# Two transformer blocks on one core: down and output products with the activations stationary, and token-major norms

## The chip, the cores and the metric

The kernel runs on one core of one Trainium2 chip. The metric is device time in microseconds (us), the median of several executions. A profile is one more execution, taken by the hardware profiler, and its span runs from the first to the last instruction of the core.

## What is computed

The reference runs 256 tokens of width 1024 through two blocks of two layers each, in float32. A layer of the first block has three sublayers (feed-forward, mixer, feed-forward), each followed by a residual and a layer norm; a layer of the second has a mixer and a convolutional feed-forward.

```python
# first block, l = 0, 1
y = swiglu(modulate(x, mod[:, 0, 0], mod[:, 0, 1]), ffn_w13[l, 0], ffn_w2[l, 0])
x = layer_norm(ALPHA * x + 0.5 * (1 + mod[:, 0, 2])[:, None, :] * y, ln_g[l, 0], ln_b[l, 0])
y = token_mixer(modulate(x, ...), w_in[l], w_out[l], ...)
x = layer_norm(ALPHA * x + (1 + mod[:, 1, 2])[:, None, :] * y, ln_g[l, 1], ln_b[l, 1])
...
# second block, l = 0, 1 (h = layer_norm_2(x, ln_in_g, ln_in_b) ahead of it)
mix = jnp.concatenate([da_o, hg_o, mx_o], axis=-1) @ w_out
x = layer_norm_2(DEEPNORM_ALPHA * x + mix, ln1_g, ln1_b)
u = depthwise_conv_centred(x @ w_up, conv_w, conv_b)
gate, val = jnp.split(u, 2, axis=-1)
return layer_norm_2(DEEPNORM_ALPHA * x + (jax.nn.silu(gate) * val) @ w_down, ln2_g, ln2_b)
```

`layer_norm` takes mean and variance over the 1024 features of a token, then a gain and a bias by feature. The feed-forward width is 2816.

## The kernel before

**Layout.** Activations are feature-major: a tile of 128 partitions holds 8 groups (KT) of 128 features by 256 tokens (S). Weights come from memory in chunks of 128 x 2048 (1 MB), issued by SyncE (SP in the profile) into a ring of three raw buffers, in the order in which the products take them.

**Products.** Every float32 product is three products of a shorter format: an operand is cast to a high part and the rest is its low part, and hi·hi, lo·hi and hi·lo are added up in PSUM. `Chunk.hi` (L247, ScalarE) and `Chunk.lo` (L255, VectorE) split a weight chunk; `split` (L530, L531) splits activations; `mm3` (L425 to L427) issues the three products. In all of these 128 x 128 of the weights is stationary and 256 tokens of activations move past it, so that features come out on partitions. `gemm_a` (L550 to L553) is the same for the projections into a sublayer, with its own order. One projection group per mixer (L852) moves 408 columns.

**Down.** The class `Down` (L267) makes the product that ends a sublayer: the feed-forward's second matrix (11 chunks, `ffn` L556), the mixers' output matrix (4 chunks in `mixer1` L828, 6 in `mixer2`). A chunk gives 8 feature groups x 2 halves x 3 products of 256 columns, 48 matmuls, into 4 PSUM banks `y`, each bank holding two feature groups. The last two chunks are taken group by group, so that the groups finish one after the other.

**The norm.** `norm` (L706) adds `y`, times the gate in the first block, to the scaled residual `xa` (VectorE, L714 or L716). `sums` (L667) makes the sums over features: ScalarE squares (L680), VectorE adds up the first feature groups (L684, L685), and TensorE adds up across partitions and the remaining groups with a matrix of 1/1024 (L688; plain float32, two array passes per matmul). Mean and 1/deviation then stand on all partitions for each token. `scaled` (L721) subtracts the mean (L698) and multiplies (L723) group by group on VectorE; `make_xf` (L477) makes of each group, with gain, bias and the next sublayer's modulation as scale and bias by partition, the high part `xh` and the full `xm` (both ScalarE, L480) and the low part `xl` (VectorE, L484). The next sublayer's products start on group 0 as soon as it is there. Between the blocks two norms follow each other (`norm_again` L732). `residual` (L746, called by `keep` early in the next sublayer) makes `xa` from the normed tile on ScalarE (L741). The last norm writes out through `dump` (L1641).

**Work beside the norms.** `filler` and `kv_chunk` (L617 to L645) hold eight chunks of products of `mem` with a later mixer's weights. `program` (L1651) gives one chunk (48 matmuls) to each of the norms (0,0), (0,1), (0,2), (1,0), (1,1) and (2,1), and two to (1,2), the double norm. (l,s) is the norm behind sublayer s of layer l of the first block; (2,1) is the one behind the second block's first feed-forward. The two norms behind `mixer2` and the last norm have none. A scheduler sets the order in which each engine gets its instructions from priorities; the diff does not spell it out.

Of the kernel before, what the change touches and what calls it, by code (L numbers as in the profile page):

```python
# [10 lines left out]
F32 = mybir.dt.float32  # L11
# [7 lines left out]
P = 128  # L19
D = 1024  # L20
# [50 lines left out]
def _consts():  # L71
# [17 lines left out]
    out = [[("ident", np.eye(P)), ("mean", np.full((P, P), 1.0 / D)), ("ones", np.ones((P, P))), ("zeros", np.zeros((P, 8)))],  # L89
# [97 lines left out]
def host_pack(i):  # L187
# [10 lines left out]
    a["xT"] = np.ascontiguousarray(i["x"][0].T.reshape(KT, P, S).transpose(1, 0, 2).reshape(P, KT * S))  # L198
    a["c"] = np.ascontiguousarray(i["c"])
# [67 lines left out]
class Down:  # L267


    def __init__(self, net, y, n):  # L270
        self.net, self.y, self.n, self.i = net, y, n, 0

    def add(self, c, hh, hl):
        i, n = self.i, self.n
        self.i += 1
        if i == n - 2:
            self.kept = (i, c, hh, hl)
        for f in range(KT):
            if i < n - 1 and (f < 4 or i < n - 2):
                self.part(f, i, c, hh, hl)  # L280
            elif i == n - 1:
                if f >= 4:
                    self.part(f, *self.kept)
                self.part(f, i, c, hh, hl)

    def part(self, f, i, c, hh, hl):
        for kk in range(2):
            self.net.mm3(self.y[f // 2][:, (f % 2) * S:(f % 2 + 1) * S], *c(kk * D + f * P, P), hh[kk], hl[kk],
                         i == 0 and kk == 0 and f % 2 == 0, i == self.n - 1 and kk == 1 and f % 2 == 1)
# [20 lines left out]
class Net:  # L310
    def __init__(self, ctx, tc, a, soff, off):
# [9 lines left out]
        self.xap = ent(tc.tile_pool(name="xap", bufs=1))  # L321
# [33 lines left out]
    def constants(self, pool, j):  # L355

        nc = self.nc
        for kind, dt in (("consts", F32), ("masks", U8), ("sels", F32R)):
# [6 lines left out]
            if dt == F32:  # L365
                nc.sync.dma_start(t, src)
            else:
                with self.tc.tile_pool(name="mskf", bufs=1) as tmp:
                    f = tmp.tile([P, n], F32, name="mskf")[:m]
                    nc.sync.dma_start(f, src)  # L370
                    nc.vector.tensor_copy(t, f)
# [105 lines left out]
    def make_xf(self, f, src, A, B, xh, xl, between=lambda: None, late=False):  # L477
        nc = self.nc
        t = self.temp("xm")
        to = lambda t: self.pin(nc.scalar.activation(out=t, in_=src[:, f], func=AF.Identity, scale=A[:, f:f + 1], bias=B[:, f:f + 1]), late)  # L480
        to(xh[:, f])
        between()
        to(t)
        self.pin(nc.vector.tensor_tensor(out=xl[:, f], in0=t, in1=xh[:, f].bitcast(F32), op=ALU.subtract), late)  # L484

    def make_x(self, src, A, B, each):
        xh, xl = self.new_x()
        for f in range(KT):
            each(f)
            self.make_xf(f, src, A, B, xh, xl)  # L490
            self.between(f)
        return xh, xl

    def start(self, c1, w, ada):
# [6 lines left out]
        with ExitStack() as ctx:  # L501
# [3 lines left out]
            for f in range(KT):  # L505
# [16 lines left out]
                self.make_xf(f, r, mod[:, 8:16], mod[:, 0:8], xh, xl, rest, True)  # L522
# [4 lines left out]
        return r, xh, xl, small  # L527
# [28 lines left out]
    def ffn(self, wa, wb, xh, xl, conv, extra, fill, made=()):  # L556

        nc = self.nc
        with ExitStack() as ctx:
# [7 lines left out]
            for g in range(NG):  # L567
# [36 lines left out]
                extra(g, side)  # L604
                if fill and g == 3:
                    mem = self.memory(side, *(F.tile([P, KT, S], F32R, bufs=1, tag=t, name=t) for t in ("memh", "meml")))
            down.add(*held.pop())
            yield y, pwt, self.filler(mem, F, pwt) if fill else no_fill
# [58 lines left out]
    def sums(self, r, each, st, direct=6):  # L667


        nc = self.nc  # L670
        v, mm = nc.vector, nc.tensor.matmul
        new = self.temp
        self.table(RSQRT)
        s1, s2 = new("s1"), new("s2")
        st = st()
        parts = [(s1, s2)]
        for f in range(KT):
            each(f)
            q = s2 if f == 0 else new("sq")
            nc.scalar.activation(out=q, in_=r[:, f], func=AF.Square)  # L680
            if f >= direct:
                parts.append((r[:, f], q))
            elif f > 0:
                v.tensor_tensor(out=s1, in0=s1 if f > 1 else r[:, 0], in1=r[:, f], op=ALU.add)  # L684
                v.tensor_tensor(out=s2, in0=s2, in1=q, op=ALU.add)  # L685
        for i, p in enumerate(parts):
            for j in range(2):
                mm(st[:, j * S:(j + 1) * S], self.cs("mean"), p[j], start=i == 0 and j == 0, stop=i == len(parts) - 1 and j == 1)  # L688
        self.between(-1)
        t, y, u, mean = new("lnt"), new("lny"), new("lnu"), new("s1")  # L690
        nc.scalar.activation(out=t, in_=st[:, :S], func=AF.Square)
        v.scalar_tensor_tensor(out=t, in0=st[:, S:], scalar=LN_EPS, in1=t, op0=ALU.add, op1=ALU.subtract)
        v.tensor_copy(mean, st[:, :S])
        nc.scalar.activation(out=y, in_=t, func=AF.Abs_reciprocal_sqrt)

        def center(f):
            if f < KT:
                self.pin(v.tensor_tensor(out=r[:, f], in0=r[:, f], in1=mean, op=ALU.subtract))  # L698
        center(0)
        nc.scalar.activation(out=u, in_=y, func=AF.Square)  # L700
        v.scalar_tensor_tensor(out=u, in0=u, scalar=-0.5, in1=t, op0=ALU.mult, op1=ALU.mult)
        center(1)
        v.scalar_tensor_tensor(out=y, in0=u, scalar=1.5, in1=y, op0=ALU.add, op1=ALU.mult)
        return y, center

    def norm(self, y, gate, res, st, fill, A=None, B=None, done=lambda r, f: None):  # L706

        v = self.nc.vector
        r = self.rp.tile([P, KT, S], F32, tag="r", name="r")

        def each(f):
            yf = y[f // 2][:, (f % 2) * S:(f % 2 + 1) * S]
            if gate is None:
                v.tensor_tensor(out=r[:, f], in0=yf, in1=res[:, f], op=ALU.add)  # L714
            else:
                v.scalar_tensor_tensor(out=r[:, f], in0=yf, scalar=gate[:, f:f + 1], in1=res[:, f], op0=ALU.mult, op1=ALU.add)  # L716
        rs = self.sums(r, each, st)
        fill()
        return r, self.scaled(r, *rs, A, B, lambda f: done(r, f))

    def scaled(self, r, rs, center, A, B, done=lambda f: None):  # L721
        def each(f):
            self.nc.vector.tensor_tensor(out=r[:, f], in0=r[:, f], in1=rs, op=ALU.mult)  # L723
            center(f + 2)
            done(f)
        if A is None:
            for f in range(KT):
                each(f)
            return None
        return self.make_x(r, A, B, each)  # L730

    def norm_again(self, r, g, b, st, fill, A, B):  # L732

        each = lambda f: self.nc.scalar.activation(out=r[:, f], in_=r[:, f], func=AF.Identity, scale=g[:, f:f + 1], bias=b[:, f:f + 1])
        rs = self.sums(r, each, st, 3)
        fill()
        return self.scaled(r, *rs, A, B)

    def affine(self, src, A, B, dst, f, act):
        if act:  # L740
# [1034 lines left out]
```

## Time and profile before

| what | us |
|---|---|
| median of 3 runs | 2069.29 (2068.16 to 2069.84) |
| profiled execution, its own time | 2064.67 |
| its span | 2062.9 |
| TensorE (PE) busy | 2011.7 of the span, 16076 instructions |
| VectorE (DVE) busy | 1596.4, 3028 instructions |
| ScalarE (ACT) busy | 1160.7, 1918 instructions |
| mean granted TensorE clock | 0.996 of full speed |
| DMA | 400.72 MB, 194 GB/s in the mean |

The profiled execution is 4.6 us under the median. Its span leaves 1.8 us of its time outside. Matmuls are pipelined, so a matmul's own duration is longer than the distance to the next one; that distance, start to start, is what a matmul costs. The row of PE clock digits on the page is 9 throughout, in 40 slices of 52 us.

### The profile page before, as it was taken

To read this page: it belongs to the slowest core of one execution; us is meant where nothing else is said; L and a number is where in the kernel's file an instruction comes from. 1 tells how busy PE (TensorE), PEld (TensorE's weight loads), DVE (VectorE), ACT (ScalarE), POOL (GpSimd) and SP (SyncE) were. 2 spreads that over 40 slices of the span, in tenths; PEclk is the share of its full clock that TensorE was granted. 3 is DMA by queue.
4 is the path that set the end of the run, shared out by engine and by line. 5 is a ranking of instruction groups with operands and counts; after the bars stand their busy time and mean duration, and the time that the engine had idled before them with its cause. 6 is when DMAs were issued, how large, how long until landed. Compare 5 with 4: busy or idle time off the path is not lost.

```text
span 2062.9 us, 39007 instructions
## 1 busy us (share of the span) xinstructions
PE 2011.7 (98%) x16076; PEld 1962.6 (95%) x16076; DVE 1596.4 (77%) x3028; ACT 1160.7 (56%) x1918; POOL 10.4 (1%) x18
## 2 busy tenths in 40 slices
PE   8999999999999999999999999999999999999997
PEld 7999989899999999999999999999899999989997
DVE  7877898987778775997886459786877697868775
ACT  4644734674447444735574448564765585648554
POOL 0000000000000000000000000000000000000000
PEclk9999999999999999999999999999999999999999
DMA  9785444478875783433377533434465343336541
GB/s 392 302 340 220 169 144 154 146 265 309 306 266 220 305 314 139 169 129 109 122 268 276 182 128 138 141 124 164 158 224 185 108 166 133 117 123 212 198 164 40
DMA packets 59445, 400.72 MB, mean 194 GB/s; under 512 B 6786, under 2 KB 8450, under 8 KB 12291
## 3 DMA queue, kind: packets, MB, share of 16 engines
q1 hardware_dynamic: 59266, 398.23, 52.9%
q8 instruction: 126, 2.06, 0.4%
q14 instruction: 53, 0.43, 0.1%
HBM read 395.05 MB, written 3.15 MB: 193 GB/s over the span
## 4 chain that ended last, share of the span: by engine, by line
PE 90%; DVE 5%; ACT 3%; issue 1%; DMA 0%; SPq 0%; ACTq 0%; DVEq 0%
PE pw L425 14%; PE pw L427 14%; PE pw L426 14%; PE y L425 6%; PE y L427 6%; PE y L426 6%; PE pw L550 3%; PE pw L551 3%; PE pw L553 3%; PE py L1529 2%; PE py L1113 1%; PE py L1107 1%; PE pw L778 1%; PE pw L780 1%; PE pw L779 1%; PE pz L425 1%
## 5 line engine op out<-in xcount | busy, mean ns | idle before, releaser
L255 DVE TENSOR_TENSOR lo<-raw,hi 128x1024 fp32r<-128x1024 f32 (+1 forms) x588 | 705.8, 1214 | 285.3 <-ACT hi L247 283.3
L247 ACT CAST hi<-raw 128x1024 fp32r<-128x1024 f32 (+1 forms) x588 | 601.6, 1041 | 436.7 <-PE pw L427 307.3
L425 PE MATMUL pw<-xh,hi 128*128 128x256 f32 x2536 | 724.2, 286 | 2.3 <-DVE zo L925 2.3
L427 PE MATMUL pw<-xl,hi 128*128 128x256 f32 x2536 | 720.7, 284 | 0.0
L426 PE MATMUL pw<-xh,lo 128*128 128x256 f32 x2536 | 720.3, 284 | 0.0
L425 PEld LDWEIGHTS pw<-xh,hi 128*128 128x128 f32 x2536 | 485.7, 192 | 4.8 <-DVE zo L925 2.4
L426 PEld LDWEIGHTS pw<-xh,lo 128*128 128x128 f32 x2536 | 485.7, 192 | 0.6
L427 PEld LDWEIGHTS pw<-xl,hi 128*128 128x128 f32 x2536 | 485.7, 192 | 0.5
L425 PE MATMUL y<-hh,hi 128*128 128x256 f32 x1056 | 296.3, 283 | 2.3 <-ACT hh L530 1.8
L426 PE MATMUL y<-hh,lo 128*128 128x256 f32 x1056 | 296.9, 283 | 0.5 <-DVE lo L255 0.5
L427 PE MATMUL y<-hl,hi 128*128 128x256 f32 x1056 | 296.3, 282 | 0.1
L425 PEld LDWEIGHTS y<-hh,hi 128*128 128x128 f32 x1056 | 200.9, 191 | 3.2 <-ACT hh L530 2.2
L426 PEld LDWEIGHTS y<-hh,lo 128*128 128x128 f32 x1056 | 201.6, 191 | 0.7 <-DVE lo L255 0.7
L427 PEld LDWEIGHTS y<-hl,hi 128*128 128x128 f32 x1056 | 201.4, 191 | 0.3 <-DVE hl L531 0.3
L453 DVE CUSTOM_DVE_ANT_0 raw<-raw,cb 128x1024 f32<-128x1024 f32 x144 | 171.7, 1219 | 18.7 <-DMA raw<-ada 12.7
L550 PE MATMUL pw<-xh,hi 128*128 128x256 f32 x464 | 118.3, 290 | 18.4 <-ACT xh L480 15.9
L551 PE MATMUL pw<-xh,lo 128*128 128x256 f32 x464 | 116.8, 288 | 0.0
L550 PEld LDWEIGHTS pw<-xh,hi 128*128 128x128 f32 x464 | 89.5, 197 | 21.6 <-ACT xh L480 18.5
L551 PEld LDWEIGHTS pw<-xh,lo 128*128 128x128 f32 x464 | 89.5, 197 | 0.3 <-DVE lo L255 0.2
L530 ACT CAST hh<-h 128x512 fp32r<-128x512 f32 x66 | 40.9, 620 | 68.6 <-DVE h L594 68.0
L553 PE MATMUL pw<-xl,hi 128*128 128x256 f32 x464 | 77.7, 286 | 0.4 <-DVE xl L484 0.4
L553 PEld LDWEIGHTS pw<-xl,hi 128*128 128x128 f32 x464 | 65.4, 193 | 1.2 <-DVE xl L484 1.2
(450 smaller groups left out, 3029.6 us busy)
## 6 DMA issues: line engine op xcount, KB each, us to landing
raw<-w SPq DMA_DIRECT2D x132, 1024.0 KB, 6.8
raw<-ada SPq DMA_DIRECT2D x72, 1024.0 KB, 4.9
raw<-win SPq DMA_DIRECT2D x62, 1024.0 KB, 4.9
raw<-wup SPq DMA_DIRECT2D x44, 1024.0 KB, 5.1
raw<-wdn SPq DMA_DIRECT2D x22, 1024.0 KB, 4.9
raw<-wo SPq DMA_DIRECT2D x12, 1024.0 KB, 4.9
raw<-wkv SPq DMA_DIRECT2D x8, 1024.0 KB, 4.9
raw<-wout SPq DMA_DIRECT2D x8, 1024.0 KB, 5.0
```

The lines of the kernel that those rows point to most:

```text
L247: self.net.pin(self.net.nc.scalar.copy(t[:, :m], self.raw[len(self.parts)]), late)
L255: self.net.pin(self.net.nc.vector.tensor_tensor(out=t[:, :m], in0=self.raw[i], in1=h[:, :m].bitcast(F32), op=ALU.subtract), late)
L425: mm(out, wh, xh, start=start, stop=False)
L426: mm(out, wl, xh, start=False, stop=False)
L427: mm(out, wh, xl, start=False, stop=stop)
L453: i = nc.vector.tensor_tensor_reduce(out=t[:, j * D:(j + 1) * D], in0=t[:, j * D:(j + 1) * D], in1=self.cb, scale=1.0, scalar=0.0, op0=ALU ...
L530: self.pin(self.nc.scalar.copy(hi, src), late)
L550: mm(o, wh, xh[:, k], start=k == 0 and n == 0, stop=False)
L551: mm(o, wl, xh[:, k], start=False, stop=False)
L553: mm(p[:, n * S:(n + 1) * S], wh, xl[:, k], start=False, stop=k == KT - 1 and n == 1)
L778: mm(out, ah, wh, start=k == 0, stop=False)
L1529: mm(p[:, (2 * j + c) * P:(2 * j + c + 1) * P], k, r, start=True, stop=True)
```

## The change

`Down` is turned round: the activations (128 features x 128 tokens) are stationary, and the weights move 512 columns at a time, so `y` comes out token-major, one PSUM bank for 128 tokens x 512 features. A chunk is 24 matmuls. The last two chunks are taken so that tokens 0 to 127 finish first (`y` banks 0 and 1), then bank 2, then bank 3.

The norm becomes token-major. The residual `r` is one resident tile of 128 x 2 x 1024. VectorE multiplies by the gate, adds and takes statistics (`bn_stats`, `bn_aggr`); VectorE and ScalarE share the normalising; TensorE transposes 16 blocks of 128 x 128 per norm back to feature-major ("flips", L744); ScalarE makes `xh` (L768) from PSUM, VectorE `xm` (L769) and `xl` (L770). The residual's gain and bias are now rows that lie along the free dimension, so they are loaded as rows broadcast to 128 partitions (`rows`, 1 MB, ten of them), and the gates are written to memory and read back broadcast (`row`, 512 KB, six of them). The input `x` is loaded token-major as well (1 MB). The constant 1/1024 goes, and the identity is used. `sums`, `scaled`, `norm_again`, `make_x` and `affine` go.

```diff
 class Down:
     def add(self, c, hh, hl):
         i, n = self.i, self.n
         self.i += 1
-        if i == n - 2:
-            self.kept = (i, c, hh, hl)
-        for f in range(KT):
-            if i < n - 1 and (f < 4 or i < n - 2):
-                self.part(f, i, c, hh, hl)
...
+        self.kept.append((i, c, hh, hl))
+        if i < n - 2:
+            for t in range(2):
+                self.part(t, (0, 1))
+        elif i == n - 1:
+            self.part(0, (0, 1))
+            for j in range(2):
+                self.part(1, (j,))
+        if i != n - 2:
+            self.kept = []
+
+    def part(self, t, columns):
+        mm = self.net.nc.tensor.matmul
+        for i, c, hh, hl in self.kept:
+            for kk in range(2):
+                h, l = (x[kk][:, t * P:(t + 1) * P] for x in (hh, hl))
+                w = [(self.y[2 * t + j], *c(kk * D + j * 512, 512)) for j in columns]
+                for y, wh, _ in w:
+                    mm(y, h, wh, start=i == 0 and kk == 0, stop=False)
+                for y, _, wl in w:
+                    mm(y, h, wl, start=False, stop=False)
+                for y, wh, _ in w:
+                    mm(y, l, wh, start=False, stop=i == self.n - 1 and kk == 1)
...
+    def normal(self, y, gate, again=None):
...
+        for t in range(2):
+            r = self.r[:, t]
+            bn = self.stats()
+            for j in range(2):
+                c, p = slice(j * 512, (j + 1) * 512), y[2 * t + j]
+                if gate is not None:
+                    v.tensor_tensor(out=p, in0=p, in1=gate[:, c], op=ALU.mult)
+                v.tensor_tensor(out=r[:, c], in0=p, in1=r[:, c], op=ALU.add)
+                v.bn_stats(out=bn[:, j], in_=r[:, c])
+            mean, rs, nb = self.deviation(bn)
...
+            for j in range(4):
+                x = r[:, j * 256:(j + 1) * 256]
+                if j % 2 == 0:
+                    v.tensor_scalar(out=x, in0=x, scalar1=mean, scalar2=rs, op0=ALU.subtract, op1=ALU.mult)
+                else:
+                    sc.activation(out=x, in_=x, func=AF.Identity, scale=rs, bias=nb)
+
+    def feature_major(self, banks, fill, each):
...
+        for f in range(KT // 2):
+            flip(0, f)
+        fill()
+        ps += [bank(k) for k in banks[2:]]
+        for f in range(KT // 2, KT):
+            flip(0, f)
         for f in range(KT):
...
+            flip(1, f)
+        for f in range(KT):
+            each(f, ps[f // 2][:, f % 2 * S:(f % 2 + 1) * S])
...
+        def each(f, p):
+            t = self.temp("xm")
+            a, b = A[:, f:f + 1], B[:, f:f + 1]
+            nc.scalar.activation(out=xh[:, f], in_=p, func=AF.Identity, scale=a, bias=b)
+            nc.vector.tensor_scalar(out=t, in0=p, scalar1=a, scalar2=b, op0=ALU.mult, op1=ALU.add)
+            nc.vector.tensor_tensor(out=xl[:, f], in0=t, in1=xh[:, f].bitcast(F32), op=ALU.subtract)
+            self.between(f)
...
+    def residual(self, rows):
 
         v = self.nc.vector
...
+            v.scalar_tensor_tensor(out=r, in0=r, scalar=ALPHA, in1=rows[0], op0=ALU.mult, op1=ALU.mult)
+            v.scalar_tensor_tensor(out=r, in0=rows[1], scalar=ALPHA, in1=r, op0=ALU.mult, op1=ALU.add)
```

`deviation` (L692) is `bn_aggr` (L698), a reciprocal square root on ScalarE (L699) and four VectorE operations on one column (L700 to L703), for each half of the tokens.

TensorE, the first down product of a feed-forward, before (`hh`, `hl`: the activations' parts; `hi`, `lo`: the weights'; the last name is the moving operand's or the stationary one's, the shape is the moving one's):

```order
L425 MATMUL y<-hh,hi 128x256 x4
L426 MATMUL y<-hh,lo 128x256
L427 MATMUL y<-hl,hi 128x256
L425 MATMUL y<-hh,hi 128x256
L426 MATMUL y<-hh,lo 128x256
L427 MATMUL y<-hl,hi 128x256
L425 MATMUL y<-hh,hi 128x256
```

The same place with the change:

```order
L300 MATMUL y<-hi,hh 128x512 x2
L302 MATMUL y<-lo,hh 128x512 x2
L304 MATMUL y<-hi,hl 128x512 x2
L300 MATMUL y<-hi,hh 128x512 x2
L302 MATMUL y<-lo,hh 128x512 x2
```

The operands have changed places, there are half as many matmuls, and each is twice as wide.

TensorE at the norm behind the first mixer, before (`py<-mem` is the filler; `py<-s` the sums with 1/1024):

```order
L427 MATMUL pw<-mhl,hi 128x256
L688 MATMUL py<-s_4843,consts_841 128x256
L425 MATMUL py<-mem,hi 128x256
L426 MATMUL py<-mem,lo 128x256
L427 MATMUL py<-mem,hi 128x256
```

And with the change (`pt<-consts,res` are the flips):

```order
L304 MATMUL pw<-hi,mhl 128x512
L300 MATMUL pw<-hi,mhl 128x512
L302 MATMUL pw<-lo,mhl 128x512
L304 MATMUL pw<-hi,mhl 128x512
L744 MATMUL pt<-consts_795,res 128x128 x4
L441 MATMUL py<-mem,hi 128x256
L442 MATMUL py<-mem,lo 128x256
L443 MATMUL py<-mem,hi 128x256
```

Four flips of the first 128 tokens stand between the last product and the filler; the other twelve stand behind the filler's 48 matmuls, ahead of the next projection.

VectorE in the same norm, before, from the reciprocal of the deviation on:

```order
L703 SCALAR_TENSOR_TENSOR lny<-lnu,lny 128x256
L723 TENSOR_TENSOR r<-r,lny 128x256
L698 TENSOR_TENSOR r<-r,s_4894 128x256
L723 TENSOR_TENSOR r<-r,lny 128x256
L698 TENSOR_TENSOR r<-r,s_4894 128x256
L723 TENSOR_TENSOR r<-r,lny 128x256
L484 TENSOR_TENSOR xl<-xm,xh 128x256
```

And with the change, from the end of the second half's statistics on (`lo<-raw` is the split of the next sublayer's weights):

```order
L703 SCALAR_TENSOR_TENSOR dev<-dev 128x1
L734 TENSOR_SCALAR res<-res,dev 128x256 x2
L259 TENSOR_TENSOR lo<-raw,hi 128x1024 x2
L783 SCALAR_TENSOR_TENSOR res<-res,rows 128x1024
L769 TENSOR_SCALAR xm<-pt,mab 128x256
L784 SCALAR_TENSOR_TENSOR res<-rows,res 128x1024
L770 TENSOR_TENSOR xl<-xm,xh 128x256
L769 TENSOR_SCALAR xm<-pt,mab 128x256 x2
L770 TENSOR_TENSOR xl<-xm,xh 128x256
```

The residual's two operations on the first half (L783, L784, 1024 columns each) now stand ahead of the first `xl`.

## Rows read from the trace of the kernel before

**Rows 1.** The page's busy times by engine.

```profile
PE 2011.7 (98%) x16076; PEld 1962.6 (95%) x16076; DVE 1596.4 (77%) x3028; ACT 1160.7 (56%) x1918; POOL 10.4 (1%) x18
```

**Rows 2.** The page's chain of work that ended last, share by engine.

```profile
PE 90%; DVE 5%; ACT 3%; issue 1%; DMA 0%; SPq 0%; ACTq 0%; DVEq 0%
```

**Rows 3.** Window 450:620: busy PE PEld DVE ACT POOL, clock, DMA share, GB/s.

```profile
450.00:620.00 170.00, 170.00 (x1422) 170.00 (x1421) 128.14 (x171) 82.30 (x99) 0.00 (x0) 1.00 0.79 297
```

**Rows 4.** Timeline of TensorE at 100 us: start, duration, instruction; 256 columns.

```profile
100.10 0.28 PE L426 MATMUL pw<-xh,lo 128*128 128x256 f32 x1
100.22 0.28 PE L427 MATMUL pw<-xl,hi 128*128 128x256 f32 x1
```

**Rows 5.** Timeline of TensorE at 218 us, 408 columns.

```profile
218.10 0.35 PE L852 MATMUL pw<-lo,xh 128*128 128x408 f32 x1
...
218.66 0.35 PE L852 MATMUL pw<-lo,xh 128*128 128x408 f32 x1
```

**Rows 6.** Timeline of TensorE, plain float32: sums (two passes each) and transposes.

```profile
1307.79 0.60 PE L1579 MATMUL pz<-consts,e 128*128 128x128 f32 x4
...
1447.94 0.59 PE L688 MATMUL py<-sq,consts 128*128 128x256 f32 x2
1448.37 0.59 PE L688 MATMUL py<-r,consts 128*128 128x256 f32 x2
```

**Rows 7.** Groups by line and shape: busy, mean ns | idle before, releaser.

```profile
L255 DVE TENSOR_TENSOR lo<-raw,hi 128x1024 fp32r<-128x1024 f32 x576 | 695.1, 1221 | 284.1 <-ACT hi L247 282.1
L531 DVE TENSOR_TENSOR hl<-h,hh 128x512 fp32r<-128x512 f32 x66 | 45.4, 688 | 15.5 <-ACT hh L530 15.5
L484 DVE TENSOR_TENSOR xl<-xm,xh 128x256 fp32r<-128x256 f32 x80 | 33.4, 421 | 5.7 <-ACT xm L480 5.2
L480 ACT ACTIVATE xh<-r,mab 128x256 fp32r<-128x256 f32 x40 | 23.9, 597 | 8.9 <-DVE r L723 8.9
L1600 DVE TENSOR_SCALAR mx<-mx 128x2 f32<-128x2 f32 x16 | 2.5, 163 | 0.0
```

**Rows 8.** Timeline of TensorE: last down product and first projection at (0,0).

```profile
203.71 0.28 PE L427 MATMUL y<-hl,hi 128*128 128x256 f32 x1
...
211.94 0.35 PE L852 MATMUL pw<-hi,xh 128*128 128x408 f32 x1
```

**Rows 9.** The same two at (0,1).

```profile
422.49 0.28 PE L427 MATMUL pw<-mhl,hi 128*128 128x256 f32 x1
...
432.34 0.39 PE L550 MATMUL pw<-xh,hi 128*128 128x256 f32 x1 [1.02 <-ACT kvo L642]
```

**Rows 10.** The same two at (1,2), the double norm.

```profile
1233.58 0.28 PE L427 MATMUL y<-hl,hi 128*128 128x256 f32 x1
...
1254.86 0.38 PE L550 MATMUL pw<-xh,hi 128*128 128x256 f32 x1 [1.23 <-ACT xh L480]
```

**Rows 11.** The same two behind the first mixer2, a norm without filler.

```profile
1446.52 0.28 PE L427 MATMUL pw<-xl,hi 128*128 128x256 f32 x1
...
1453.81 0.58 PE L550 MATMUL pw<-xh,hi 128*128 128x256 f32 x1 [4.42 <-ACT xh L480]
```

**Rows 12.** Busy time by window there.

```profile
1452.00:1454.00 2.00, 0.19 (x1) 0.19 (x2) 1.97 (x6) 0.84 (x2) 0.00 (x0) 0.51 0.00 0
1454.00:1458.90 4.90, 4.90 (x24) 4.90 (x25) 4.90 (x14) 4.90 (x9) 0.00 (x0) 0.50 0.00 0
```

**Rows 13.** The same two at (2,1).

```profile
1647.67 0.28 PE L427 MATMUL y<-hl,hi 128*128 128x256 f32 x1
...
1657.15 0.28 PE L550 MATMUL pw<-xh,hi 128*128 128x256 f32 x1
```

**Rows 14.** Timeline of the end: last down product, and the last ScalarE work.

```profile
2047.38 0.28 PE L427 MATMUL y<-hl,hi 128*128 128x256 f32 x1
...
2054.77 5.12 ACT L741 ACTIVATE r<-r,small 128x256 f32<-128x256 f32 x8 [1.62 <-DVE r L723]
```

**Rows 15.** The page's DMA issues: tile, queue, count, KB each, us to landing.

```profile
raw<-w SPq DMA_DIRECT2D x132, 1024.0 KB, 6.8
```

More of the change, by code (lines that the diff above doesn't have):

```diff
@@ L483, in make_xf @@
         to(t)
[L484 to L492, printed above, removed]
+        self.pin(nc.vector.tensor_tensor(out=xl[:, f], in0=t, in1=xh[:, f].bitcast(F32), op=ALU.subtract))
     def start(self, c1, w, ada):
@@ L604, in ffn @@
                 extra(g, side)
+                if gate is not None and g == NG - 3:
+                    gate = self.row(gate, F.tile([P, D], F32, bufs=1, tag="gate", name="gate"))
                 if fill and g == 3:
@@ L721, in scaled @@
[L721 to L737, printed above, removed]
@@ new lines, in norm @@
+    def norm(self, y, gate, banks, fill, A, B, again=None):
+        nc = self.nc
+        self.normal(y, gate, again)
+        self.between(-1)
+        xh, xl = self.new_x()
+        def each(f, p):
[5 more added lines that the diff above has]
+            self.between(f)
+        self.feature_major(banks, fill, each)
+        return xh, xl
@@ L1032, in mixer1 @@
             upto(27)
+            gate = self.row(gate, self.rp.tile([P, CH], F32, tag="r", name="gate")[:, :CH // 2])
             norm = self.mlstm_norm(l, W, mq, zo, py)
@@ L1682, in program @@
         n.psum(ph, "wwwwyyyy")
-        r, xh, xl, small = n.start(c1, a["w13_00"], ada)
-        xa = g = b = None
+        xh, xl, small = n.start(c1, a["w13_00"], ada)
+        rows = None
         def rest():
-            nonlocal g, b
+            nc.sync.dma_start(n.r, a["xr"])
             n.constants(n.const, 0)
-            g, b = n.cs("ones")[:, :KT], n.cs("zeros")
             next(small)
@@ L1702, in beside @@
                     extra(ring)
[L1703 removed]
+            return n.ffn(wa, wb, xh, xl, conv, beside, key in fills, gate, made)
         def keep():
[L1706 to L1707 removed]
+            n.residual(rows)
         for l in range(2):
@@ L1732, in program @@
                         n.ahead(*((w13(l, 1), *TIGHT) if s == 1 else (win1(l), *GATES) if s == 0 else (w13(1, 0), *ROOM)))
-                        r, (xh, xl) = n.norm(y, mod[:, 16:24], xa, st, more, *nxt)
+                        xh, xl = n.norm(y, gate, "yyyy" if s == 2 else "yyww", more, *nxt)
+                        rows = n.rows(3 * l + s)
                     next(run, None)
```

197 lines of the change are left out of this document (91 added, 106 removed).

## The prediction

> **What bounds the kernel now.** I read the busy times first: TensorE is busy for 98% of the span, VectorE for 77%, ScalarE for 56% [rows 1]. The chain that ended last says that this is no accident of overlap: 90% of it is TensorE, 5% VectorE, and DMA 0% [rows 2]. Inside a feed-forward it is stricter still: of 170 us TensorE is busy 170, at full clock, while VectorE has 42 us to spare and DMA is 0.79 busy [rows 3]. So a product costs what its matmuls cost start to start, and the other engines count only where TensorE runs dry. That is at the norms, and at the end.
>
> **Products.** A matmul of 256 columns follows the one before it after 0.12 us [rows 4]. The down and output products are 48 such matmuls a chunk: 6 feed-forwards of 11 chunks and mixers of 2 x 4 and 2 x 6 chunks, 86 chunks, 4128 matmuls. They become 2064 of 512 columns, each in place of two that cost 240 ns.
>
> No instruction of 512 columns in this format is in the rows. The nearest is 408 wide: three steps in 0.56 us, 187 ns each [rows 5]. From 256 to 408 columns, 152 more cost 67 ns, 0.44 ns a column; on that line 512 columns cost 187 + 104 x 0.44 = 233. If what 408 columns cost above the column rate of the fastest stream stayed fixed, a little less. The fastest stream is plain float32: two matmuls of 256 columns with two passes each start 0.43 us apart, 215 ns a pass of 256 columns [rows 6], which is 430 ns for 512 column steps at half rate, that is 215 for 512 at full rate and 172 for 408. By that 408 columns carry 15 ns of overhead, and 512 cost 215 + 15 = 230. I take 231, nearest to the 408 wide rows: 9 ns x 2064 = **18.6 us gained**. The bounds are 215 (no overhead left: 25 x 2064 = 51.6 gained) and 240 (a column costs what it costs at 256: nothing gained).
>
> The Trainium skill (TensorE: Matmul & The Clock Gate, Back-to-back issue gap) gives an isolated gap of columns / 2.4 GHz + 2.5 ns, that is 216 ns at 512 and 109 at 256. By its own two figures the merging would bring only about 2.5 ns x 2064 = 5 us; the row shows 120 at 256, so rule and row differ there, and with the row's 240 against the page's 216 the sum would be 50 us.
>
> The splitting of weights on ScalarE and VectorE (1221 ns a 1024 wide low part [rows 7]) is as before.
>
> **Norms.** For each I compare the time from the last down product to the next projection with the matmuls of filler in it (48 x 0.12 = 5.76 us); the rest is what the norm costs TensorE's useful work. Before: (0,0) 8.23 - 5.76 = 2.5 [rows 8]; (0,1) 9.85 - 5.76 = 4.1 [rows 9]; (1,2) 21.28 - 11.52 = 9.8 [rows 10]; mixer2 7.3, no filler [rows 11]; (2,1) 9.48 - 5.76 = 3.7 [rows 13]; the end 2062.9 - 2047.4 = 15.5 [rows 14]. (1,0) goes with (0,0), (1,1) with (0,1).
>
> Prices after, from the nearest rows: VectorE on 512 columns 0.65 us (688 ns with two operands [rows 7]; `bn_stats` stands in no row, bounds 0.42, a 256 wide operation, and 1.22, a 1024 wide one), a 256 wide operation 0.42, an operation on a column or two 0.165, ScalarE on 256 columns 0.6 [rows 7], a transpose 0.11 (four in 0.60 us with the drain [rows 6]).
>
> (0,1): banks 0 and 1 are ready 18 products, 4.2 us, ahead of the last. VectorE needs ten 512 wide operations (6.5) and five small ones (0.8) before the first half's deviation stands, so TensorE, which has four flips next, waits 7.3 - 4.2 + 0.6 (normalising) = 3.7. Then flips 0.4, filler 5.8, of which the second half's statistics and normalising are hidden, twelve flips of which the first eight go on to `xh` (0.65 + 0.6 + 0.3 to be read): 11.4 - 5.8 = 5.7. The first `xl` stands behind L783, L769 and L784 on VectorE: 1.22 + 0.42 + 1.22 + 0.42 = 3.3 after the first half's flips, so TensorE, when the `xh` products that are there are used up, waits another 1.4: 7.1, against 4.1. The same at (1,1): **+6.0**. (2,1) has only 12 products between and comes to 7.4 against 3.7: **+3.7**. At (0,0) and (1,0) the filler is parted by the flips (21 and 27 matmuls) and covers the first half's chain; there the two waits for `xl` and one low part of weights remain, 2.0 + 1.2 + 2.0 of flips and reads = 5.2 against 2.5: **+5.4** for both. (0,2) has its filler parted likewise and a little more of it ahead: nothing; its cover is those 24 matmuls, and without them it would be like (0,0). (1,2): two statistics chains now run on VectorE by halves of tokens, with 72 matmuls of filler ahead of the flips, and TensorE makes no sums: 6.6, **-3.2**. Mixer2 has no cover: the chain of 7.3 us before becomes 2 x 0.65 after the last bank, statistics 0.8, normalising 1.0, sixteen flips 1.8, `xh` 0.6 and the VectorE queue 2.5: 8.0, **+1.4** for both. The end: two 512 wide operations, 0.8, 1.0, flips 1.3, then `dump` alternates ScalarE and VectorE, some 2.8, and the last store 3.0 (ScalarE ended at 2059.9, the span at 2062.9 [rows 14]), with drains 11.0: **-4.5**. Sum: **+8.8 us**.
>
> **Clock.** Behind mixer2 TensorE is idle for 4.42 us, and its granted clock is 0.50, the 1.2 GHz level, until 1458.9; the 24 matmuls in those 4.9 us would take 2.9 at 2.4 GHz, a loss of 2.0 us [rows 11, 12]. The new waits at (0,1), (1,1) and (2,1) are 3.7 and 1.4 us: near it. I put in one such fall, **+2.0**; the bounds are none and three.
>
> **Costed at nothing.** Ten loads of `rows`, six of gates, one of x, some 14 MB on SP's queue, each with weight loads behind it. A 1 MB load lands in 6.8 us [rows 15], while a chunk's 48 matmuls last 5.8 us and three chunks are in the ring; the gate's write and its read back are one wait of about a landing. Without that cover each would cost up to 6.8 us. ScalarE gets lighter (no squares, no `xm`, no `xa`); it bounds nothing.
>
> Sum: -18.6 + 8.8 + 2.0 = **-7.8**: the profiled 2064.7 would be 2056.9. The median of the runs shown is 4.6 us higher, so I forecast 2069.3 - 7.8 = 2061.5, say **2061 us**.
>
> **Rivals.** (1) Wide matmuls cost 215. For: the plain float32 passes show that a stream without gaps exists, and with half as many stationary loads the queue gets shorter. Against: the overhead did not shrink from 256 (120 - 108 = 12 ns) to 408 (15 ns). Time: -51.6 + 10.8 = -40.8, 2028.5.
>
> (2) Slower: VectorE at the inner norms. The residual's L783 needs `rows`, whose load waits at (0,1) for the gate's last use in the same buffer and lands 6.8 us later; everything behind L783 on VectorE, the `xl` first, waits with it, and TensorE with that. If this, or the whole residual (four operations of 1.22) and a low part of weights ahead of `xl`, costs 3 us more at each of nine inner norms: +27 - 7.8 = +19.2, 2088.5. It decides from 7.8 / 9 = 0.9 us a norm on. For: the order has L783 and L784 ahead of the first `xl`. Against: 5.8 us of filler pass before.
>
> (3) No change: the clock. It falls at six norms rather than one, since TensorE has only short work around the flips: five more at 2.0 us, -7.8 + 10 = +2.2, 2071.5. For: the one long idle shows it [rows 12]. Against: the waits are shorter than 4.4 us and parted by filler. The Trainium skill (TensorE: Matmul & The Clock Gate, PE-mode transpose) says that transposes do not count as busy for the clock; no run here shows a norm with them. That the operands change places without effect is excluded: the order shows half the matmuls.
>
> **How the numbers follow.** About 0.2% (4.1 us) can be told from no change. Forecast 0.52, its own range 2047 to 2069 (a price of 226 to 233, and 4 us either way for the norms); 0.05 of it lies within 0.2%. Rival 1 0.15, rival 2 0.20, rival 3 0.13. Faster: 0.47 + 0.15 = 0.62; same 0.05 + 0.13 = 0.18; slower 0.20. The range reaches to rival 1 and takes in the milder half of rival 2: **2027 to 2079**.
>
> **What would show it.** In the profile of the changed kernel: matmuls of 512 columns 231 ns apart in `y`; about 14,000 TensorE instructions (16076 less 2064, less the sums, plus 160 flips); TensorE waiting at the first flips for VectorE's or ScalarE's normalised `res` at (0,1), (1,1), (2,1), some 3 to 4 us, and for `xl` afterwards, 1 to 2; the span ending 11 us after the last product. Wrong it would be if the wide matmuls were 215 or 240 apart, if the norms lost more than 18.6 us, or if a weight load or `rows` came late: then the releaser of a long idle of VectorE or TensorE would be a DMA.

## The result, and the profile after

The changed kernel takes 2101.86 us (median of 4 runs, 2100.18 to 2107.36) against 2068.72 before (the three runs of the table above and one more): 1.0168 times as long, 95% interval 1.0145 to 1.0191. 2061 was forecast, with a range up to 2079: wrong in sign.

The profiled execution has a span of 2098.1 us. The page's span line, its busy times, the row of clock digits and the chain's shares (the busy times answer to [rows 1], the chain to [rows 2]):

```profile
span 2098.1 us, 34651 instructions
PE 2000.7 (95%) x14028; PEld 1867.1 (89%) x14028; DVE 1620.1 (77%) x2984; ACT 1061.2 (51%) x1694; POOL 10.4 (0%) x18
...
PEclk9999999999999999999999999999899999998999
...
PE 88%; DVE 7%; ACT 2%; DMA 2%; issue 1%; SPq 0%; ACTq 0%; DVEq 0%
```

TensorE is busy 11 us less, in a span that is 35.2 us longer: about 46 us more of standing still. Two of the clock digits are 8 now. The view of the cores gives the mean, 0.996 before:

```profile
core 0: 2098.1 us, clock 0.980
```

A mean of 0.980 with two levels means 2 x 0.020 x 2098 = 84 us at 1.2 GHz, to the rounding of the mean; before it was 2 x 0.004 x 2063 = 17.

TensorE in a feed-forward's down product, answering to [rows 4] (timeline):

```profile
639.66 0.39 PE L304 MATMUL y<-hi,hl 128*128 128x512 f32 x1
639.89 0.39 PE L300 MATMUL y<-hi,hh 128*128 128x512 f32 x1
...
641.02 0.39 PE L304 MATMUL y<-hi,hl 128*128 128x512 f32 x1
```

Six steps in 1.36 us: 227 ns a matmul of 512 columns, 13 less than two of 256. The products brought their gain, 2064 x 13 ns = 26.8 us, and more than forecast.

The waits of TensorE, by group and releaser: total, times, longest.

```profile
PE pw L558 <- DVE xm L769: 31.1, 6, 6.5
PE pt L744 <- DVE res L734: 21.7, 8, 4.1
PE pw L881 <- DVE xm L769: 10.9, 2, 5.5
```

The second row was expected: the first transposes wait for normalised data. The first and third were not. At eight norms the next sublayer's first projection (L558, or L881 behind the feed-forwards (0,0) and (1,0)) waits 42 us in all, and not for its operand `xh`, which ScalarE makes, but for VectorE's `xm`, which TensorE never reads. The norm (0,1) in the timeline, to be held against [rows 9]; TensorE first, then VectorE, then ScalarE's first `xh`:

```profile
434.63 0.40 PE L304 MATMUL pw<-hi,mhl 128*128 128x512 f32 x1
438.25 0.75 PE L744 MATMUL pt<-consts,res 128*128 128x128 f32 x4 [3.22 <-DVE res L734]
446.02 1.47 PE L744 MATMUL pt<-consts,res 128*128 128x128 f32 x12
453.11 0.55 PE L558 MATMUL pw<-xh,hi 128*128 128x256 f32 x1 [5.62 <-DVE xm L769]
```

```profile
446.66 1.23 DVE L783 SCALAR_TENSOR_TENSOR res<-res,rows 128x1024 f32<-128x1024 f32 x1 [3.01 <-PE pt L744]
447.80 0.54 DVE L769 TENSOR_SCALAR xm<-pt,mab 128x256 f32<-128x256 f32 x1
448.26 1.22 DVE L784 SCALAR_TENSOR_TENSOR res<-rows,res 128x1024 f32<-128x1024 f32 x1
...
449.72 0.99 DVE L769 TENSOR_SCALAR xm<-pt,mab 128x256 f32<-128x256 f32 x2
...
452.43 0.99 DVE L769 TENSOR_SCALAR xm<-pt,mab 128x256 f32<-128x256 f32 x2
```

```profile
446.88 0.56 ACT L768 ACTIVATE xh<-pt,mab 128x256 fp32r<-128x256 f32 x1
```

The first wait, 3.2 us, comes out as forecast (3.7). The second does not: TensorE starts at 453.11, 0.15 us behind the end of the fourth `xm` (the first of the pair at 452.43), though the first `xh` was there at 447.4. Between 434.63 and 453.11 there are 18.5 us, 9.9 before.

Windows of that place (busy times, granted clock, DMA share, GB/s), to be held against [rows 12]:

```profile
439.00:442.50 3.50, 3.50 (x19) 3.50 (x19) 2.87 (x10) 2.32 (x4) 0.00 (x0) 0.51 0.11 42
447.30:453.10 5.80, 0.19 (x2) 0.02 (x1) 5.80 (x11) 5.80 (x10) 0.00 (x0) 0.96 0.71 220
452.50:456.25 3.75, 3.14 (x15) 3.17 (x16) 3.75 (x7) 2.40 (x4) 0.00 (x0) 0.54 0.14 20
```

Behind each of the two waits the clock falls to 1.2 GHz, for 3.4 us each.

By place, from the last down product to the next projection (starts in the timelines of both kernels; the values before are those of [rows 8] to [rows 14]):

| place | before | after | difference |
|---|---|---|---|
| (0,0), (1,0) | 8.2, 8.4 | 13.3, 13.4 | +10.0 |
| (0,1), (1,1) | 9.9, 9.9 | 18.5, 18.7 | +17.4 |
| (0,2) | 9.4 | 9.8 | +0.4 |
| (1,2) | 21.3 | 19.7 | -1.6 |
| behind mixer2, twice | 7.3 each | 13.6 each | +12.6 |
| (2,1) | 9.5 | 15.4 | +5.9 |
| the end | 15.5 | 11.0 | -4.5 |
| all between these | | | -5.0 |

The sum is +35.2. The inner norms lose 44.7; the stretches between them gain 5.0 where the products alone should give 26.8. One norm is nearly free: (0,2), the only one whose next sublayer is a feed-forward behind a feed-forward.

### The profile page after: what moved, and what is told of

Its sections match the earlier page's. It is cut to its first block, busy times and chain, and to the rows that moved or that the text cites. A ratio compares the mean times of both kernels' runs of the same rounds, so it can differ in the third digit from the quotient of the medians.

```text
span 2098.1 us, 34651 instructions
## 1 busy us (share of the span) xinstructions
PE 2000.7 (95%) x14028; PEld 1867.1 (89%) x14028; DVE 1620.1 (77%) x2984; ACT 1061.2 (51%) x1694; POOL 10.4 (0%) x18
## 4 chain that ended last, share of the span: by engine, by line
PE 88%; DVE 7%; ACT 2%; DMA 2%; issue 1%; SPq 0%; ACTq 0%; DVEq 0%
PE pw L441 13%; PE pw L443 13%; PE pw L442 13%; PE y L300 5%; PE y L302 5%; PE y L304 5%; PE pw L558 3%; PE pw L559 3%; PE pw L561 3%; PE py L1559 1%; DVE lo L259 1%; PE pw L807 1%; PE pw L809 1%; PE pw L808 1%; PE py L1143 1%; PE py L1137 1%
## 5 line engine op out<-in xcount | busy, mean ns | idle before, releaser
L441 PE MATMUL pw<-xh,hi 128*128 128x256 f32 x2432 | 693.5, 285 | 0.0
L442 PE MATMUL pw<-xh,lo 128*128 128x256 f32 x2432 | 692.2, 285 | 0.0
L443 PE MATMUL pw<-xl,hi 128*128 128x256 f32 x2432 | 691.2, 284 | 0.0
L443 PEld LDWEIGHTS pw<-xl,hi 128*128 128x128 f32 x2432 | 466.2, 192 | 0.5
L300 PE MATMUL y<-hi,hh 128*128 128x512 f32 x528 | 168.3, 393 | 5.1 <-ACT hi L251 3.6
L302 PE MATMUL y<-lo,hh 128*128 128x512 f32 x528 | 167.5, 391 | 0.0
L304 PE MATMUL y<-hi,hl 128*128 128x512 f32 x528 | 167.1, 391 | 0.0
L558 PE MATMUL pw<-xh,hi 128*128 128x256 f32 x464 | 125.3, 301 | 37.7 <-DVE xm L769 31.1
L558 PEld LDWEIGHTS pw<-xh,hi 128*128 128x128 f32 x464 | 95.0, 208 | 41.1 <-issue 32.7
L559 PE MATMUL pw<-xh,lo 128*128 128x256 f32 x464 | 123.5, 299 | 0.0
L302 PEld LDWEIGHTS y<-lo,hh 128*128 128x128 f32 x528 | 99.1, 188 | 21.8 <-DVE lo L259 0.8
L304 PEld LDWEIGHTS y<-hi,hl 128*128 128x128 f32 x528 | 99.4, 188 | 21.2
L300 PEld LDWEIGHTS y<-hi,hh 128*128 128x128 f32 x528 | 95.4, 189 | 23.3 <-ACT hi L251 4.2
L561 PE MATMUL pw<-xl,hi 128*128 128x256 f32 x464 | 80.3, 293 | 1.3 <-DVE xl L770 1.3
L561 PEld LDWEIGHTS pw<-xl,hi 128*128 128x128 f32 x464 | 69.0, 203 | 1.5 <-DVE xl L770 1.5
```

Of the source, the lines that this page charges most:

```text
L300: mm(y, h, wh, start=i == 0 and kk == 0, stop=False)
L302: mm(y, h, wl, start=False, stop=False)
L304: mm(y, l, wh, start=False, stop=i == self.n - 1 and kk == 1)
L441: mm(out, wh, xh, start=start, stop=False)
L442: mm(out, wl, xh, start=False, stop=False)
L443: mm(out, wh, xl, start=False, stop=stop)
```

## The experiments

**The theories.** *Banks*: each sublayer takes its PSUM (and SBUF) from pools of its own, laid out anew. In a string such as `zzzyyyww` each letter stands for one of the eight PSUM banks, in order, and the banks of one letter are one pool. The theory is that a new pool that overlaps an old one waits until the old pool's last reader is done. No trace shows the banks; what follows is read from the layout. In the program as built, the transposes of (0,1) fill banks 3, 4, 6 and 7; the first projection writes bank 0, which none of them filled, but its pool covers banks 0 to 3, and the pool of the first two transposed tiles (groups 0 to 3) covered 3 to 5. The last reader of that pool is `xm` of group 3. At (1,2) and (2,1) only groups 0 and 1 lie in the overlapped pool, and TensorE starts 0.15 us behind `xm` of group 1. Between (0,2) and (1,0) the layout stays, and there is no such wait. (The expectation below speaks of the projection's own bank; by the layout it is the pool.) *Queue*, the rival: VectorE is late anyway, with L783, L784 and low parts ahead of `xm` and `xl`. For the clock: *idle* (it falls because TensorE stands still) against *transposes* (because they do not count as work).

### Other banks

```diff
-n.psum(ph, "zzzyyyww" if s == 1 else "wwwwyyyy")
+n.psum(ph, "zzzyyyww" if s == 1 else "yyyywwww")
...
-xh, xl = n.norm(y, gate, "yyyy" if s == 2 else "yyww", more, *nxt)
+xh, xl = n.norm(y, gate, "yzzz" if s == 1 else "yyyy", more, *nxt)
```

and likewise at the other norms: `"yzzz"` behind mixers, `"yyyy"` behind feed-forwards.

> The PSUM pools of a feed-forward are laid out in the other order and the transposes put into other banks, so that the first projection's bank is no longer one that the transposes filled. Nothing else is changed. Bank theory (the projection waits until VectorE's xm of group 3, or 1, has read the transposes out of that bank): the wait before the first projection falls from 5.5 us to about 1 at the eight norms that have it (0.15 us behind the first xh), 35 to 40 us in all, and with shorter waits half of the clock falls go, 5 to 10 us more: 2055 to 2070 us. Queue theory (VectorE is late anyway, by the residual's two operations and the low parts ahead of xl): the projection starts earlier but stops after its first matmuls for xl, and the time stays above 2090.

Measured: 2073.05 us, 1.0030 (1.0019 to 1.0042) of before: 28.8 us less than the change, and a little above the 2055 to 2070 expected. The waits:

```profile
PE pt L744 <- DVE res L734: 18.9, 7, 4.1
PE pw L558 <- DVE xm L769: 12.8, 4, 3.5
...
PE pw L881 <- DVE xl L770: 4.3, 4, 1.4
...
PE pw L561 <- DVE xl L770: 3.0, 3, 1.3
```

and the norm (0,0) in the timeline:

```profile
219.44 1.47 PE L744 MATMUL pt<-consts,res 128*128 128x128 f32 x12
220.91 0.45 PE L881 MATMUL pw<-hi,xh 128*128 128x408 f32 x1
```

The projection follows the last transpose at once; the wait of 5.5 us is gone and (0,0) takes 7.9 us. The four waits that stay are those behind the mixers, where one transposed tile still lies in an overlapped pool: they fell from 5.6 to about 3, the distance from `xm` of group 3 to that of group 1. VectorE's order at (0,1) is the same, so the queue theory, which wanted over 2090, falls for these 29 us. It is right in a small part: at (0,0) and (1,0) the projection now stops for `xl` after its first matmuls, as that theory said, for some 2 us each. Up to the first projection the inner norms now lose 12.7 us; the waits for `xl` behind it, 7.3 us against 0.4 before, come on top.

### The residual later

```diff
-v.scalar_tensor_tensor(out=r, in0=r, scalar=ALPHA, in1=rows[0], op0=ALU.mult, op1=ALU.mult)
+self.pin(v.scalar_tensor_tensor(out=r, in0=r, scalar=ALPHA, in1=rows[0], op0=ALU.mult, op1=ALU.mult))
```

and the same for the second operation.

> The residual's operations L783 and L784 are kept in program order, so that they stand behind the norm's xm and xl instead of between them. Nothing else is changed. Queue theory: the wait before the first projection loses the two operations that stand ahead of xm of group 3, 2 x 1.2 us, at seven norms, 17 us, and some clock falls with it: 2075 to 2085. Bank theory: the same 17 us at the most, and the projection still starts 0.15 us behind xm of group 3, not behind xh.

Measured: 2117.6 us, 1.0238 (1.0211 to 1.0265): 16 us slower than the change. The waits for `xm` fell only from 42.0 to 36.0 us, and the inner chains of two mixers lost as much. Waits of TensorE:

```profile
PE pw L558 <- DVE xm L769: 27.7, 6, 6.2
...
PE py L1137 <- DVE D L1127: 9.2, 6, 1.8
```

The second was 2.9 us in the changed kernel; 4.6 us of it now fall in each of the first block's two mixers, some 30 us behind the moved residual. The residual's 4.9 us of VectorE had a cheap place beside the transposes. That its new place in the mixers causes these waits is likely but not shown. The profiled execution is the fastest of the four (2108.09), so it does not show where more than half of the 16 us went. The queue theory's remedy is worse than the ill.

### The filler first

```diff
+        fill()
+        ps += [bank(k) for k in banks[2:]]
-        for f in range(KT // 2):
+        for f in range(KT):
             flip(0, f)
-        fill()
...
```

> All of the filler stands ahead of all 16 transposes, where four transposes stood ahead of it or in it. Nothing else is changed. If TensorE loses time ahead of the first transposes because VectorE's statistics are late there (3.6 us at (0,1) and (1,1), 3.3 at (2,1), 2 to 3 at (0,0), (1,0)), the filler now covers it: 12 to 16 us less, and the clock falls ahead of the filler at (0,1) and (1,1) go: 2080 to 2088. If the end of VectorE's chain sets the norm whatever TensorE does before, no change: 2098 to 2104.

Measured: 2088.57 us, 1.0101 (1.0086 to 1.0116): 13.3 us less than the change, within the 12 to 16 expected. (0,1), (1,1) and (2,1) fall from 18.5, 18.7 and 15.4 us to 15.0, 14.5 and 10.3; (0,0) and (1,0) keep their 13.4, since the scheduler had put 21 products ahead of the transposes already. The mean clock is no better (0.979): the falls ahead of the filler at (0,1) and (1,1) go, but longer ones stand at the projection, where the wait for `xm` grew to 7.3 us.

### Two halves for each wide matmul

```diff
-                for y, wh, _ in w:
-                    mm(y, h, wh, start=i == 0 and kk == 0, stop=False)
+                for y, wh, _ in w:
+                    for b in q:
+                        mm(y[:, b], h, wh[:, b], start=i == 0 and kk == 0 and b is q[0], stop=False)
```

with `q` the slices 0 to 256 and 256 to 512, and the same for the other two products.

> Each product of 512 columns is issued as two of 256, with the same stationary operand and the same banks. Price theory: 227 ns become 240, 2064 x 13 ns = 27 us more, 2129. Rival: the wide matmuls themselves lower the granted clock (falls that before did not have, at 401 and 425 us inside the first mixer), then those falls go and the time rises by less than 20 us.

Measured: 2122.92 us, 1.0268 (1.0251 to 1.0285): 21.1 us above the change. The halves follow each other after 120 ns, so the price holds. The time rose by less than the 27 us, but not by less than 20, and the clock was no better (0.977). Of the two falls inside the first mixer the one near 401 us stayed (at 407), so it does not need the wide form; the one near 425 did not show, and one near 308 came up. Where the missing 6 us went is open.

### Products, or transposes, in the long wait

Behind the last transpose of (0,0), (0,1), (1,0) and (1,1), with a PSUM tile that nobody reads:

```diff
+            for i in range(44):
+                self.pin(nc.tensor.matmul(p[:, :S], fill.mem[:, i % KT, :P], fill.mem[:, i % KT], start=i == 0, stop=i == 43))
```

> The changed kernel, and 44 more products of 256 columns (5.3 us at the 2.4 GHz level), whose result nobody reads, behind the last transpose of the norms (0,0), (0,1), (1,0) and (1,1), where TensorE waited 5.6 us. Idle theory of the clock: the granted clock falls because TensorE stands still there, so the falls right behind those four norms (at 220, 452, 852 and 1074 us) go and the time is 4 to 8 us less in spite of 176 more matmuls. If the transposes ahead are the cause, the falls stay, the extra products run at the 1.2 GHz level and make the wait longer: 0 to 10 us more.

and in the second run

```diff
+            for i in range(48):
+                self.pin(nc.tensor.transpose(p[:, i % 4 * P:(i % 4 + 1) * P], self.cs("ident"), self.cs("ident")))
```

> As the run before, with 48 more transposes of the identity (5.2 us) in place of the 44 products, at the same four places. If a TensorE that transposes is busy to the clock gate as one that multiplies, the result is that of the run before. If transposes do not count, the falls at 220, 452, 852 and 1074 us stay although TensorE has no gap, and the time is that of the changed kernel, 2098 to 2106.

Measured: 2093.8 us (1.0127, 1.0110 to 1.0144) and 2092.67 us (1.0124, 1.0110 to 1.0138): 8 and 9 us less than the change, with 176 matmuls and 192 transposes more. The timeline and the window of (0,1), with products and then with transposes:

```profile
441.13 5.51 PE L780 MATMUL idle<-mem 128*128 128x256 f32 x44
446.99 0.36 PE L558 MATMUL pw<-xh,hi 128*128 128x256 f32 x1 [0.36 <-DVE xm L771]
...
446.90:453.00 6.10, 6.01 (x50) 6.04 (x51) 6.10 (x11) 2.30 (x4) 0.00 (x0) 1.00 0.88 318
```

```profile
442.49 5.40 PE L780 MATMUL idle<-consts 128*128 128x128 f32 x48
448.27 0.36 PE L558 MATMUL pw<-xh,hi 128*128 128x256 f32 x1 [0.38 <-DVE xm L771]
...
446.90:453.00 6.10, 5.72 (x49) 5.51 (x47) 6.10 (x12) 3.71 (x5) 0.00 (x0) 1.00 0.31 93
```

Still released by `xm`, but after a wait of 0.4 us, and the clock stays at 2.4 GHz. The fall behind the first wait (3.2 us, not filled) stays in both. It is standing still that costs the clock, and plain float32 transposes keep it as well as products do. The Trainium skill (TensorE: Matmul & The Clock Gate, PE-mode transpose) says that a transpose does not count as busy for the clock in the same way, with figures for bf16; for float32 transposes as this kernel issues them this pair of runs shows otherwise.

### The banks, with the residual behind the last xl

```diff
+        with self.tc.issue_after(self.made.ins):
...
```

> The banks of the first experiment, and the residual's operations issued behind the norm's last xl (by order alone, nothing else is held back). Queue theory, for what is left after the banks: 2.4 us at each of the two norms behind mixer2, where L783 and L784 stand in the second half's statistics, 1.2 to 2.4 at (0,1) and (1,1) ahead of xm of group 1, and some xl: 8 to 14 us less than the first experiment, 2059 to 2065. If they only fill a time in which VectorE would wait, no change: 2070 to 2076.

Measured: 2072.66 us (1.0019, 1.0007 to 1.0032), no change against the 2073.05 with banks alone, and outside the 2059 to 2065 expected for the queue theory. The profiled execution is the slowest of the ten (2078.58). The norms behind mixer2 fall from 10.9 to 8.2 us each, and the stretch up to the first of them grows by 5.8. What VectorE does not do at the norm it does in the sublayer, where TensorE waits as well.

### The same, with the filler first at two norms and x loaded later

> The run before, and the filler ahead of the transposes at (0,1) and (1,1), and the load of x for the residual issued two steps later in the first feed-forward. Filler: 3 us and a clock fall of 1.7 at each of the two norms. Load: if its 1 MB on the busy queue is what holds up the first down product (3.6 us of waiting for hi, and a fall behind it), 4 to 5 us in the first stage, else nothing there. 2046 to 2056 in all: faster than both kernels.

Measured: 2066.51 us (0.9991, 0.9977 to 1.0004): level with before. The filler gave its part ((0,1) and (1,1) at 10.8 and 11.0 us). The time expected, 2046 to 2056, was not reached. The later load gave nothing: the first down product waits 3.6 us as before, so this load on SP's queue is not what holds it up.

### Banks and filler, the residual moved behind mixer2 alone

The first experiment, `fill()` ahead of the transposes behind `mixer1`, and `issue_after` with the second `xl`, behind `mixer2` only.

> The banks of the first experiment, the filler ahead of the transposes at (0,1) and (1,1), and the residual's operations behind the norm's second xl at the two norms behind mixer2 alone (elsewhere as in the first experiment). The first experiment stands at 2073. Filler: 3.6 us of waiting and a clock fall of 1.7 at two norms, 8 to 10 us. Mixer2: the second half's statistics without L783 and L784, 2.4 us at two norms, 5 us. 2058 to 2064. If the residual there only moves a cost into the feed-forward behind, 2063 to 2068.

Measured: 2060.24 us, 0.9959 (0.9948 to 0.9970): faster than both kernels.

### Transposes in the waits that are left

```diff
+        if banks[1] == "z" and not early_fill:
+            self.warm(34)
         for f in range(KT):
             flip(1, f)
+        if banks[1] == "z":
+            self.warm(26)
```

> The run before, and transposes of the identity that nobody reads in the waits that are left at the four norms behind a mixer: 34 ahead of the second half's transposes behind mixer2 (3.7 us), 26 behind the last one of each (2.8 us). If idle TensorE is what lowers the clock, the falls at 443, 1061, 1467 and 1866 us go and the time is 6 to 12 us below the run before; if they only lengthen the waits, it is 0 to 4 us above it.

Measured: 2054.28 us, 0.9930 (0.9917 to 0.9942): 6 us less by 172 transposes whose results nobody reads (60 at each norm behind `mixer2`, 26 at each behind `mixer1`), and the fastest version. The granted clock behind the first mixer2 (window, columns as above):

```profile
1455.00:1475.00 20.00, 19.94 (x170) 19.70 (x169) 19.47 (x29) 11.77 (x17) 0.00 (x0) 1.00 0.39 138
```

### The gate's buffer, and the kernel before with transposes

In the changed kernel and in each run so far the first down product waits 3.6 us, near 63 us. ScalarE's timeline of the changed kernel ahead of it:

```profile
59.95 1.08 ACT L602 ACTIVATE h<-pw 128x512 f32<-128x512 f32 x2 [5.87 <-PE pw L561]
```

In the program as built, the pool of the feed-forward had grown by the gate's 4 KB a partition into the pool of the first weights' high parts.

```diff
-gate = self.row(gate, F.tile([P, D], F32, bufs=1, tag="gate", name="gate"))
+gate = self.row(gate, self.rp.tile([P, CH], F32, tag="r", name="gate")[:, :D] if made else
+                                    F.tile([P, D], F32, bufs=1, tag="gate", name="gate"))
```

> The run with transposes in the waits, and in the first feed-forward the gate's 4 KB a partition are taken from the buffer of the rows instead of the feed-forward's own pool. With them that pool reached to 180032 bytes, into the pool of the first weights' high parts, which begins at 177984; without them it ends ahead of it, as before the change (176384 against 178432). Hand-over theory: a pool that overlaps an earlier one waits for that pool's last reader, here TensorE's last product of the start, so the first activation at 56 us comes 3.6 us earlier, the clock fall at 64 us goes (1.7), and the time is 4 to 6 us less: 2048 to 2051. If the loads on SP's queue hold it up, no change: 2052 to 2057.

```profile
56.65 1.08 ACT L602 ACTIVATE h<-pw 128x512 f32<-128x512 f32 x2 [2.54 <-PE pw L561]
```

The activation starts 3.3 us earlier than in the changed kernel (3.9 earlier than in the run with transposes, where it stood at 60.52), and the wait of 3.6 us is gone: the same hand-over, in SBUF. In the time it cannot be seen: 2054.87 us (2048.65 to 2057.86; 0.9933, 0.9919 to 0.9947). The six runs lie further apart than those of the run before, with mean clocks from 0.991 to 0.996, so clock falls at places that differ from run to run hide it; where they are, the one profile (2048.65) does not show.

In the kernel before, `lambda: n.warm(36)` in place of the empty filler behind `mixer2`:

> The kernel before, with 36 transposes of the identity that nobody reads (3.9 us) in the wait of 4.4 us at the two norms behind mixer2. If idle TensorE is what lowers the clock, the falls at 1452 and 1855 us go there too, 2.0 us each at the most: 2 to 4 us less than before. If the falls of the changed kernel come from something else that it does, no change here.

Measured: 2064.93 us, 0.9985 (0.9977 to 0.9994). Window to be held against [rows 12]:

```profile
1454.20:1459.00 4.80, 4.76 (x35) 4.41 (x36) 4.80 (x13) 4.80 (x9) 0.00 (x0) 1.00 0.01 3
```

The falls go there too. The clock's price is no property of the change; the change made more idle places.

## Why the prediction was wrong

**What bounds the kernel**: right. TensorE's time start to start decided each stretch, and every loss lies where it ran dry, or behind that at the lower clock.

**Products**: right in kind, too small: 227 ns, not 231; 26.8 us, not 18.6. What the prediction had as 15 ns of overhead at 408 columns is 227 - 215 = 12 at 512, as at 256. The Trainium skill's 216 for an isolated matmul (TensorE: Matmul & The Clock Gate, Back-to-back issue gap) is not reached.

**Norms**: the step that failed. It let the projection start when the first `xh` was read ("0.65 + 0.6 + 0.3 to be read") and counted VectorE only through `xl`. It did not ask who holds the PSUM pool that the projection writes. The diff shows the bank letters of the transposes, and the layouts of the sublayers stand in the same function; the overlap could have been found there. Sum forecast for the inner norms: +13.3 (8.8 with the end's -4.5). Measured: +44.7. With the banks apart it is +12.7 up to the first projection. Add the waits for `xl`, which the forecast had counted too (7.3 us against 0.4 before), and take off some 6 us that matmuls lost there at the lower clock, which it priced apart: 13.5. That this meets the 13.3 is luck, since errors of both signs cancel. In the same terms (0,1) and (1,1) lost 8.6 us together, 6.0 was forecast; the two norms behind mixer2 lost 5.1, 1.4 was forecast; (0,0) and (1,0) lost 3.4, 5.4 was forecast; (2,1) gained 2.0, a loss of 3.7 was forecast. At mixer2 the forecast's 8.0 us left out that L783 and L784 stand inside the second half's statistics: with them moved behind (the runs with 2072.66 and 2060.24 us) the norm took 8.2. The end: -4.5, as forecast.

**Clock**: +2.0 was forecast. The time at 1.2 GHz grew from 17 to 84 us. Counting for each matmul in it what it took above its distance at full clock, some 27 us were lost, against some 4 before; 7 of them lie inside the norms of the table. The 16 us more that lie between the norms are most of why the stretches there gained 5.0 and not 26.8; the rest is waits, the 3.6 us near 63 us the longest new one. The size of one fall was about right (27 us over 15 stretches are 1.8 each, 2.0 was forecast); I had one more where there are twelve more such stretches, because the waits were thought to be 1.4 us behind the transposes and were 5.6, and because waits shorter than the row of 4.42 were enough: 3.2 us at (0,1), and in the first mixer 2.3 us near 401 and 1.4 us near 425.

**Costed at nothing**: `rows` and gates on SP's queue cost nothing that shows in a wait, as said. The gate's room in SBUF cost 3.3 us at the start of ScalarE's work, which was not looked for. Leaving the residual on VectorE at nothing holds only where it stands: moving it everywhere cost as much (2072.66 against 2073.05) or more (2117.6 against 2101.86). Behind mixer2 alone it shortened the norms by 2.7 us each, in a run that also moved the filler.

**Rivals**: the second named the place (VectorE behind the transposes, nine norms, over 0.9 us each) and the sign, with 0.20. Its mechanism was not it: no L783 waited for `rows`, and with the banks apart taking L783 and L784 away everywhere brought nothing. Yet VectorE's queue had its part: the overlap makes the wait, and L783, L784 and the low parts ahead of `xm` of group 3 set how long it is. The third, the clock, was a cost beside the main one and no case of its own. The first, wide matmuls at 215, did not come.

**Open**: why the changed kernel's first mixer falls to 1.2 GHz near 401 us behind a wait of 2.3 us that the kernel before has too, and that the run with other banks has without a fall; why the halves cost 21 and not 27 us; and the spread of the run with the gate moved.

## What to carry to other kernels

When an edit gives an intermediate a new buffer in PSUM or SBUF, ask which later tile takes that memory and who reads the intermediate last; here a reader that TensorE did not need cost 29 us through a pool that overlapped. A wait of TensorE can cost more than its length, since behind the long ones here the matmuls ran at the lower clock: close the wait first, and fill what is left with matmuls that nobody reads (172 transposes gained 6 us here). A releaser in the waits that is not an operand is the sign to look for such a hand-over.

## What the runs showed of the hardware that was not expected

- A matmul of 512 columns in this format follows the last after 227 ns, 256 after 120, 408 after 187 [rows 5].
- In the changed kernel the waits of 2.9 to 6.6 us, the start aside, were each followed by 3.4 us or more at 1.2 GHz. Of shorter ones some were (1.4 us near 425 us) and some were not (1.5 us near 304).
- Transposes of plain float32 keep the clock at 2.4 GHz as products do: 172 of them, run for nothing, made the kernel 6 us faster.
- The gain from 512 wide products is real and can be had: with other banks, the filler first behind `mixer1`, the residual later behind `mixer2` and the waits behind the mixers filled, the changed kernel is at 2054.3 us, 0.9930 of before, where the kernel before with its own two waits filled is at 0.9985.
